# Hybrid attention layer: four of the output gate's eight row sums, and their weight loads, moved from z's second and fourth projection to its sixth and eighth

## The chip, the cores and the metric

The kernel runs on one core of one Trainium2 chip. The metric is the device time of one launch in microseconds (us), median of several runs. An execution taken by the hardware profiler gives the trace; its times count from the start of the span, which is the part of the launch that the trace covers. Engines are named as in the profile: PE (TensorE matmuls), PEld (its weight loads), DVE (VectorE), ACT (ScalarE), POOL (GpSimd), SP (SyncE, whose queue issues most DMAs). L764 is line 764 of the kernel before.

## The reference

One decoder layer on x of 512 tokens by 1024 features:

```
mod = silu(c) @ w_ada + b_ada ;  shift, scale, gate = split(mod, 3)
h = rms_norm(x, norm_gain) * (1 + scale) + shift
q_a,k_a,v_a,z_a, q_b,kc,vc,ks,vs,kw,vw, z_b,g_b = split(h @ w_in)
o_a = sliding-window attention (window 128, sinks) of group A, 8 heads
o_b = g0*compressed + g1*selected + g2*window-512 attention of group B, 8 heads
y = concat(o_a * silu(z_a), o_b * silu(z_b))
out = x + gate * (y @ w_out)
```

The change is about `gate`: 1024 numbers, each the dot product of silu(c) with one column of the last third of w_ada, plus its bias. They are needed only in the last line.

## The kernel before

Activations lie transposed, features on the 128 partitions, 512 tokens in a row. Every projection is made in split precision: a weight block is copied to a rounded high part `wh` (ACT, L192) and a low part `wl` (DVE, L193, weight minus `wh`), h likewise into `hh` and `hl`, and PE sums three products per block, `wh,hh`, `wl,hh` and `wh,hl` (L518 and L528). After a first stage that makes h and group A's q, k, v (to about 47 us), two things run beside each other and are interleaved on every engine:

- the **slots** of attention (`run`): 16 of group A, then 28 of group B (a slot is a pair of heads, a branch and a block of 128 queries). A slot is scores on PE (L1019 for A; L977 and L1004 for B, into PSUM tile `s`), bias and maximum on DVE (L1026; L979, L1006), exponential on ACT (L1010, L984), scaling (L1043, L1047 on DVE), transposes on PE (L1062, L1076, into `pt`), a copy on ACT (L1063, L1077), for group A a triangle mask on DVE (L1067, into `ptT`), and the product with the values on PE (L1095, into `po`), four slots at a time;
- the **stream** (`gen1`, then `gen2`): the other projections, in this order: kv_cmp, kv_sel, kv_win_g, q_b0, q_b1, then z in eight projections n = 0 to 7 (z_a0, z_a1, z_b0, z_b1, each in two halves of 128 columns). After q_b come norms and transposes for the queries of group B (`post_q`: L561 sums of squares, L114 to L121 an inverse root in small steps, L571 `qn`, L579 transposes on PE, L584 and L585 the halves `qs`).

Small pieces of work behind a projection (`posts`) are drawn one step at a time while the next projection is traced. One kind is `gate_slice(q)`: two DVE reductions (L764), each of a 128x1024 weight tile times the row `scrow` into one column of `gate`. Each starts at a raw weight tile and ends with `load_next()`.

Raw weights come through one pool `raw` of five buffers, in the fixed order `raw_order` (L160): a load for a tile goes to SP's queue and waits there until the tile five places before it has been used. What stands behind it in SP's queue waits too; among that are the bias rows of group B's heads (L966). The wh/wl pieces have four buffers each.

The order written in the code is not the final one: a scheduler places the instructions on each engine, and hoists what it thinks has time. `mark` keeps DVE instructions by name, and `in_order` ties later instructions behind one of them without a semaphore, that is, in the queue's order alone. The table `GATE` (L37) does this for the reductions n = 4 (behind `kn2`, the normalised window keys, L592) and n = 6 and 7 (behind `qn11`, the last L571).

The end (from about 256 us) is the output product, written out by hand in `TAIL`; the columns of `gate` are read there, first at 262 us.

Of the kernel before, what the change touches and what calls it, by code (L numbers as in the profile page):

```python
# [14 lines left out]
OP = mybir.AluOpType  # L15
# [18 lines left out]
NR = 4  # L34
LW = 4
PE_MODS = 2
GATE = {4: "kn2", 6: "qn11", 7: "qn11"}  # L37


TAIL = """  # L40
# [35 lines left out]
@contextmanager  # L76
def in_order(tc, after=(), only=None):

    traced = tc.nc.cur_bb.bb.instructions
    n = len(traced)  # L80
    last = dict(after)
    yield last
    info = mybir.DependencyInfo(mybir.DependencyClass.NoSync, mybir.DependencyReason.DATA)
    for i in tc.nc.cur_bb.bb.instructions[n:]:
        if only and i.engine not in only:
            continue
        if i.engine in last:
            tc.add_manual_dep(i, last[i.engine].name, info, reason="in_order")
        last[i.engine] = i
# [3 lines left out]
def hybrid_layer_kernel(ctx, tc, A, out):  # L93
    nc = tc.nc
    PE, DVE, ACT, POOL, SP = nc.tensor, nc.vector, nc.scalar, nc.gpsimd, nc.sync
# [14 lines left out]
    def rsqrt(v, n, name="n_y"):  # L110
# [15 lines left out]
    cT, prm, ident = first[:, 0:8], first[:, 8:40], first[:, 40:168]  # L126
# [30 lines left out]

    raw_order = [(g, h) for g in ("kv_cmp", "kv_sel", "kv_win_g") for h in range(2)]
    raw_order += [(f"cmp{kv}", q) for q in range(4) for kv in range(2)]
    raw_order += [(g, h) for g in ("q_b0", "gate0", "q_b1", "gate1", "z_a0", "gate2", "z_a1", "gate3", "z_b0", "z_b1",  # L160
                                   "o0", "o1", "o2", "o3") for h in range(2)]
    raws, pieces, pending = {}, {}, list(raw_order)

# [367 lines left out]
    chain, marks = {}, {}  # L531
# [227 lines left out]
    def gate_slice(q):  # L759

        for h in range(2):
            n, w = 2 * q + h, raws[f"gate{q}", h]
            with in_order(tc, {DVE.engine: marks[GATE[n]]} if n in GATE else {}, (DVE.engine,)):
                DVE.tensor_tensor_reduce(out=w, in0=w, in1=scrow, scale=0.5, scalar=prm[:, 16 + n:17 + n],  # L764
                                         op0=OP.mult, op1=OP.add, accum_out=gate[:, n:n + 1])
            load_next()
            yield 0.0

# [174 lines left out]
    def gen2():  # L943
        posts.append(cmp_attn())
        for n in range(8):
            b = PJ()
            yield from with_posts(unit_col(f"z_{'ab'[n // 4]}{n % 4 // 2}", n % 2, b))
            posts.insert(0, post_z(n, b))
            if n in (1, 3):
                posts.append(gate_slice(2 + n // 2))  # L950
        yield from flush_posts()


# [397 lines left out]
```

## Time and profile before

| what | value |
|---|---|
| time, 3 runs | median 299.51 us (299.44 to 300.15) |
| the profiled execution's own time | 299.99 us |
| its span in the trace | 297.7 us (2.29 us of the time lie around it) |
| PE busy | 290.1 us, 97% |
| PEld busy | 254.6 us, 86% |
| DVE busy | 261.0 us, 88% |
| ACT busy | 205.1 us, 69% |
| share of the chain that ended last | PE 70%, DVE 13%, DMA 10%, ACT 3% |
| the eight reductions L764 start at | 101.64, 103.76, 110.96, 114.10, 120.48, 132.56, 155.04, 169.97 us |

Granted clock of TensorE is full throughout. A PE matmul's busy time overlaps that of the next one, since they are pipelined; how far apart two matmuls start tells more than how long one is shown. Likewise a DVE instruction is shown some tens of ns longer than the step to the next start. In the timeline, a bracket behind a row gives the idle time before it and who ended it.

### The profile page before, as it was taken

To read this page: it belongs to the slowest core of one execution; us is meant where nothing else is said; L and a number is where in the kernel's file an instruction comes from. 1 tells how busy PE (TensorE), PEld (TensorE's weight loads), DVE (VectorE), ACT (ScalarE), POOL (GpSimd) and SP (SyncE) were. 2 spreads that over 40 slices of the span, in tenths; PEclk is the share of its full clock that TensorE was granted. 3 is DMA by queue.
4 is the path that set the end of the run, shared out by engine and by line. 5 is a ranking of instruction groups with operands and counts; after the bars stand their busy time and mean duration, and the time that the engine had idled before them with its cause. 6 is when DMAs were issued, how large, how long until landed. Compare 5 with 4: busy or idle time off the path is not lost.

```text
span 297.7 us, 6067 instructions
## 1 busy us (share of the span) xinstructions
PE 290.1 (97%) x2181; PEld 254.6 (86%) x2182; DVE 261.0 (88%) x730; ACT 205.1 (69%) x501; POOL 9.6 (3%) x28
## 2 busy tenths in 40 slices
PE   7999999999999999999999999999999999999995
PEld 3678888789989989989878988888888888889995
DVE  3689998999995998998999999999979779599992
ACT  5778657777848574967858567878877869567510
POOL 1000000000000100000000000000000000021210
PEclk9999999999999999999999999999999999999999
DMA  7999987842485884361402440223100120027272
GB/s 246 388 405 380 356 309 226 299 161 70 140 275 156 238 266 132 109 211 37 135 11 71 140 133 10 71 73 143 44 28 2 61 83 2 0 44 188 53 160 89
DMA packets 27417, 44.27 MB, mean 149 GB/s; under 512 B 1867, under 2 KB 18412, under 8 KB 27388
## 3 DMA queue, kind: packets, MB, share of 16 engines
q1 hardware_dynamic: 26380, 42.49, 42.2%
q0 software_dynamic: 864, 1.31, 3.0%
q8 instruction: 17, 0.28, 0.4%
q10 hardware_dynamic: 144, 0.09, 0.1%
q14 instruction: 12, 0.10, 0.1%
HBM read 41.74 MB, written 2.14 MB: 147 GB/s over the span
## 4 chain that ended last, share of the span: by engine, by line
PE 70%; DVE 13%; DMA 10%; ACT 3%; issue 2%; SPq 0%; DVEq 0%; ACTq 0%
PE pj L528 16%; PE pj L518 11%; PE po L1095 8%; PE pj L1205 6%; PE s L1004 5%; PE pt L1076 4%; DMA wst_ring<-in_w_qkv_a 4%; DMA ada_ring<-in_w_ada_rows 4%; PE s L1205 3%; PE pt L1062 3%; PE s L657 2%; DVE wl L193 2%; PE po L528 2%; DVE ada_ring L245 2%; PE s L1019 2%
## 5 line engine op out<-in xcount | busy, mean ns | idle before, releaser
L518 PE MATMUL pj<-wh,hh 128*128 128x256 f32 (+1 forms) x128 | 37.2, 291 | 0.0
L518 PE MATMUL pj<-wh,hl 128*128 128x256 f32 (+1 forms) x128 | 36.9, 288 | 0.0
L518 PE MATMUL pj<-wl,hh 128*128 128x256 f32 (+1 forms) x128 | 36.7, 287 | 0.0
L1010 ACT ACTIVATE pp<-pp,nm 128x256 f32<-128x256 f32 (+2 forms) x48 | 29.2, 610 | 6.3 <-DVE nm L1006 5.7
L528 PE MATMUL pj<-hh,wh 128*128 128x512 f32 x72 | 28.9, 402 | 0.0
L528 PE MATMUL pj<-hl,wh 128*128 128x512 f32 x72 | 28.8, 400 | 0.0
L528 PE MATMUL pj<-hh,wl 128*128 128x512 f32 x72 | 28.7, 399 | 0.0
L192 ACT ACTIVATE wh<-raw 128x512 fp32r<-128x512 f32 (+1 forms) x40 | 24.7, 635 | 5.3 <-PE pj L528 3.8
L193 DVE TENSOR_TENSOR wl<-raw,wh 128x512 fp32r<-128x512 f32 (+1 forms) x40 | 27.1, 692 | 1.4 <-ACT wh L192 1.1
L1006 DVE CUSTOM_DVE_ANT_0 pp<-s,bias 128x256 f32<-128x256 f32 (+2 forms) x48 | 25.5, 550 | 2.2 <-PE s L1004 2.0
L518 PEld LDWEIGHTS pj<-wh,hh 128*128 128x128 f32 x128 | 24.1, 189 | 0.4 <-issue 0.3
L518 PEld LDWEIGHTS pj<-wh,hl 128*128 128x128 f32 x128 | 24.2, 189 | 0.2 <-issue 0.2
L518 PEld LDWEIGHTS pj<-wl,hh 128*128 128x128 f32 x128 | 24.2, 189 | 0.1
L1004 PE MATMUL s<-kTb,qs 128*128 128x256 f32 (+2 forms) x96 | 23.6, 348 | 0.0
L1047 DVE TENSOR_SCALAR pp<-pp,rr,grev 128x256 f32<-128x256 f32 (+2 forms) x48 | 21.2, 474 | 0.3
L1004 PEld LDWEIGHTS s<-kTb,qs 128*128 128x128 f32 x96 | 16.9, 189 | 3.1 <-DVE nm L1006 0.3
L1010 ACT ACTIVATE pa<-pa,nm 128x129 f32<-128x129 f32 x32 | 12.7, 398 | 7.7 <-DVE nm L1026 6.0
L1077 ACT COPY ptT<-pt 128x384 f32<-128x384 f32 (+1 forms) x32 | 15.6, 526 | 1.1 <-PE pt L1076 1.0
L1063 ACT COPY ptT<-pt 128x256 f32<-128x256 f32 (+1 forms) x28 | 12.8, 457 | 4.1 <-PE pt L1062 3.7
L528 PEld LDWEIGHTS pj<-hh,wl 128*128 128x128 f32 x72 | 13.6, 188 | 2.4
L528 PEld LDWEIGHTS pj<-hl,wh 128*128 128x128 f32 x72 | 13.6, 189 | 2.3
L1076 PE MATMUL pt<-first,pp 128*128 128x128 f32 x112 | 15.5, 275 | 0.0
(320 smaller groups left out, 830.6 us busy)
## 6 DMA issues: line engine op xcount, KB each, us to landing
ada_ring<-in_w_ada_rows SPq DMA_DIRECT2D x12, 512.0 KB, 7.5
raw<-in_w_cmp SPq DMA_DIRECT2D x8, 512.0 KB, 6.6
raw<-in_w_gate SPq DMA_DIRECT2D x8, 512.0 KB, 4.5
raw<-in_w_o SPq DMA_DIRECT2D x8, 512.0 KB, 3.2
wst_ring<-in_w_qkv_a SPq DMA_DIRECT2D x8, 384.0 KB, 7.9
bias<-line_d SPq DMA_DIRECT2D x12, 256.0 KB, 4.0
xTp<-in_xT SPq DMA_DIRECT2D x8, 256.0 KB, 3.8
raw<-in_w_q_b SPq DMA_DIRECT2D x4, 512.0 KB, 4.8
```

Source lines behind the costliest of these rows:

```text
L192: ACT.activation(wh, src, AF.Copy)
L193: DVE.tensor_tensor(wl, src, wh.bitcast(F32), op=OP.subtract)
L518: PE.matmul(bank[:, t * n:(t + 1) * n], h[:, tb * 128:(tb + 1) * 128], w[:, k % 2, :], start=k == 0 and m == 0, stop=k == 7 and m == 2)
L528: PE.matmul(bank, w, h, start=k == 0 and m == 0, stop=k == 7 and m == 2)
L1004: PE.matmul(ps, qs[8 + 4 * g + r][:, 128 * i:128 * i + 128], kT[br, g][:, hl_, 0:w], start=hl_ == 0, stop=hl_ == 1)
L1006: DVE.tensor_tensor_reduce(out=P[:, g, 0:w], in0=ps, in1=bias["b", r, g][:, 512 - w:512], scale=1.0, scalar=3e38, op0=OP.add, op1=OP.min, ...
L1010: ACT.activation(P[:, g], P[:, g], AF.Exp, bias=nm[:, g:g + 1], scale=-1.0, accum_out=dn[:, g:g + 1])
L1047: DVE.tensor_scalar(v, v, rr[:, g:g + 1], gates[:, g, br:br + 1], op0=OP.mult, op1=OP.mult)
L1076: PE.transpose(pt[:, b * 128:(b + 1) * 128], P[:, g, b * 128:(b + 1) * 128], ident)
L1077: ACT.copy(T[:, 0:nb, :], rev(pt[:, 0:nb * 128].rearrange("p (b q) -> p b q", b=nb)))
L1095: PE.matmul(o[64 * g:64 * g + 64, 128 * i:128 * i + 128], vb[:, 64 * g:64 * g + 64], sl["T"][g][:, b, :], start=first_of and b == 0, stop= ...
L1205: PE.matmul(parts[g, p], a[:, r, :], b, start=new and r == 0 and m == 0, stop=r == 3 and m == 2, skip_group_check=True)
```

## The change

Three edits. In `raw_order` the tiles of gate2 and gate3 (four loads of 512 KB) move from between the z_a tiles to before and after z_b1. In `gen2` the two `gate_slice` calls that use them are put behind the projections n = 5 and n = 7 instead of n = 1 and n = 3. And the table GATE with its ties goes, so that all eight reductions stand where the scheduler puts them. No arithmetic changes, and the number of instructions of each kind stays the same.

```
-GATE = {4: "kn2", 6: "qn11", 7: "qn11"}
...
-    raw_order += [(g, h) for g in ("q_b0", "gate0", "q_b1", "gate1", "z_a0", "gate2", "z_a1", "gate3", "z_b0", "z_b1",
+    raw_order += [(g, h) for g in ("q_b0", "gate0", "q_b1", "gate1", "z_a0", "z_a1", "z_b0", "gate2", "z_b1", "gate3",
                                    "o0", "o1", "o2", "o3") for h in range(2)]
...
-            with in_order(tc, {DVE.engine: marks[GATE[n]]} if n in GATE else {}, (DVE.engine,)):
-                DVE.tensor_tensor_reduce(out=w, in0=w, in1=scrow, scale=0.5, scalar=prm[:, 16 + n:17 + n],
-                                         op0=OP.mult, op1=OP.add, accum_out=gate[:, n:n + 1])
+            DVE.tensor_tensor_reduce(out=w, in0=w, in1=scrow, scale=0.5, scalar=prm[:, 16 + n:17 + n],
+                                     op0=OP.mult, op1=OP.add, accum_out=gate[:, n:n + 1])
...
-            if n in (1, 3):
-                posts.append(gate_slice(2 + n // 2))
+            if n in (5, 7):
+                posts.append(gate_slice(n // 2))
```

In the changed kernel the lines stand one to two lower: the reduction is L762 there, L1067 is L1065, L518 is L517, L1004 is L1002. Up to DVE's `kn2` all engines' orders are the same as before. Behind it they part; from the instructions on that before came at about 237 us of the trace they are the same again, up to numbers of buffers.

First place: DVE behind `kn2` (`kn` in the first row), and the PE instruction that waits there. `ss_q` are sums of squares for group B's queries, `s` and `pa` belong to group A's slots. Before:

```order
L592 TENSOR_TENSOR kn<-kr,n_y 128x512
L1051 TENSOR_SCALAR pa<-pa,rr 128x128
L764 ISA raw,gate<-raw,scrow,first 128x1024
L764 ISA gate 128x1
L1043 RECIPROCAL rr<-dn 128x2
L561 TENSOR_REDUCE ss_q<-sq 128x8
L1051 TENSOR_SCALAR pa<-pa,rr 128x128
```

and now:

```order
L591 TENSOR_TENSOR kn<-kr,n_y 128x512
L1049 TENSOR_SCALAR pa<-pa,rr 128x128
L1041 RECIPROCAL rr<-dn 128x2
L1049 TENSOR_SCALAR pa<-pa,rr 128x128
L560 TENSOR_REDUCE ss_q<-sq 128x8
L1021 COPY_PREDICATED s<-rest,s 128x2x128
```

The fifth reduction is gone from here, and likewise the sixth from the small steps of q_b0's inverse root, in front of L115. The last mask product L1067 of these slots stood nine instructions behind the one before it (a masked copy L1023, four low parts, two maxima L1026 and two pieces of the window keys, L606); now one low part and one maximum lie between. On PE the last product with `va_step`, which reads its `ptT`, stood before behind eleven matmuls of q_b1's projection:

```order
L518 MATMUL pj<-wh,hh_83 128x256
L518 MATMUL pj<-wl,hh_83 128x256
L518 MATMUL pj<-wh,hl_91 128x256
L518 MATMUL pj<-wh,hh_84 128x256
L518 MATMUL pj<-wl,hh_84 128x256
L518 MATMUL pj<-wh,hl_92 128x256
L518 MATMUL pj<-wh,hh_85 128x256
L518 MATMUL pj<-wl,hh_85 128x256
L518 MATMUL pj<-wh,hl_93 128x256
L518 MATMUL pj<-wh,hh_86 128x256
L518 MATMUL pj<-wl,hh_86 128x256
L1095 MATMUL po<-ptT,va_step 64x128 x2
```

Now it is ahead of them:

```order
L1093 MATMUL po<-ptT,va_step 64x128 x2
L1093 MATMUL po<-ptT,va 64x128 x2
L1093 MATMUL po<-ptT,va_step 64x128 x2
L517 MATMUL pj<-wh,hh_83 128x256
L517 MATMUL pj<-wl,hh_83 128x256
```

Second place: DVE at q_b1's inverse root (`n_t`, `n_y`), between two low parts (`wl`) of z_a1. Before:

```order
L117 SCALAR_TENSOR_TENSOR n_y<-n_t,n_y 128x16
L118 TENSOR_TENSOR n_t<-n_y 128x16
L119 SCALAR_TENSOR_TENSOR n_t<-n_t,ss_q 128x16
L193 TENSOR_TENSOR wl<-raw,wh 128x512
L120 SCALAR_TENSOR_TENSOR n_t<-n_t 128x16
L121 SCALAR_TENSOR_TENSOR n_y<-n_t,n_y 128x16
L571 TENSOR_TENSOR qn<-pp,n_y 128x512 x2
```

Now the fifth reduction stands among them:

```order
L116 SCALAR_TENSOR_TENSOR n_y<-n_t,n_y 128x16
L117 TENSOR_TENSOR n_t<-n_y 128x16
L118 SCALAR_TENSOR_TENSOR n_t<-n_t,ss_q 128x16
L762 ISA raw,gate<-raw,scrow,first 128x1024
L762 ISA gate 128x1
L192 TENSOR_TENSOR wl<-raw,wh 128x512
L119 SCALAR_TENSOR_TENSOR n_t<-n_t 128x16
L120 SCALAR_TENSOR_TENSOR n_y<-n_t,n_y 128x16
L570 TENSOR_TENSOR qn<-pp,n_y 128x512 x2
```

The sixth stands where the eighth stood before (169.97 us of the trace). The seventh and the eighth stand behind two reciprocals L1043 of group B's second pair of heads, which before came at 189.45 and 195.71 us. So the scheduler has hoisted all four to places well ahead of the projection behind which the code puts them.

Third place: PE at the scores of group B's first 256-wide slot (two pairs, one for each key group, into the two buffers of `s`). Before, the second pair came behind the end of q_b1's projection (L518) and nine matmuls of z's first (L528), the last seven of them these:

```order
L1004 MATMUL s<-kTb_657,qs_1812 128x256 x2
L528 MATMUL pj<-hh_82,wl 128x512
L528 MATMUL pj<-hh_83,wh 128x512
L528 MATMUL pj<-hl_91,wh 128x512
L528 MATMUL pj<-hh_83,wl 128x512
L528 MATMUL pj<-hh_84,wh 128x512
L528 MATMUL pj<-hl_92,wh 128x512
L528 MATMUL pj<-hh_84,wl 128x512
L1004 MATMUL s<-kTb_659,qs_1815 128x256 x2
```

Now thirteen matmuls of q_b1 are still to come when it stands:

```order
L1002 MATMUL s<-kTb_657,qs_1812 128x256 x2
L517 MATMUL pj<-wh,hh_85 128x256
L517 MATMUL pj<-wl,hh_85 128x256
L1002 MATMUL s<-kTb_659,qs_1815 128x256 x2
L517 MATMUL pj<-wh,hl_93 128x256
```

The two pairs, and ahead of them the transposes L579 (by twelve matmuls of q_b1's projection) and the scores L977 (by nine), have moved forward in PE's queue. On DVE the four maxima L979 in front of the first 256-wide slot stood before with four low parts `wl` between or ahead of them; now these low parts come behind. In the second pair of heads (about 187 to 210 us) it is the other way round: there PE has up to thirteen more of z's matmuls ahead of the same transposes L1076 than before.

On SP's queue the loads of gate2 and gate3 now stand among those of z_b. The bias rows of the third pair of heads (L966) stood before behind the first load of w_o; now they stand behind the third of these four loads, and the fourth behind them.

## The prediction

> **What bounds the kernel now.** I read the page's busy times and its chain first, then the busy times of the stretch in which the change acts, then the timeline of PE there, and last the lists of who waited for whom.
>
> ```profile
> PE 290.1 (97%) x2181; PEld 254.6 (86%) x2182; DVE 261.0 (88%) x730; ACT 205.1 (69%) x501; POOL 9.6 (3%) x28
> PE 70%; DVE 13%; DMA 10%; ACT 3%; issue 2%; SPq 0%; DVEq 0%; ACTq 0%
> ```
>
> The busy times from 120 us (the fifth reduction) to 231 us (PE, PEld, DVE, ACT, POOL, then clock and DMA):
>
> ```profile
> 120.00:231.00 111.00, 110.36 (x851) 96.41 (x850) 105.64 (x323) 83.99 (x219) 0.60 (x3) 1.00 0.25 81
> ```
>
> PE is busy for 110.36 of 111 us, DVE for 105.64, so neither number alone settles which one sets the pace: matmuls overlap in this view. What settles it is how far apart they start. Three stretches of PE's timeline, at 129, at 151 and in the tail, where the chain holds nothing but PE:
>
> ```profile
> 129.47 0.28 PE L518 MATMUL pj<-wh,hh 128*128 128x256 f32 x1
> 129.59 0.28 PE L518 MATMUL pj<-wl,hh 128*128 128x256 f32 x1
> 130.17 0.44 PE L1095 MATMUL po<-ptT,va_step 128*64 128x128 f32 x4 [0.30 <-DVE ptT L1067]
> ...
> 151.50 0.39 PE L528 MATMUL pj<-hh,wl 128*128 128x512 f32 x1
> 151.73 0.40 PE L528 MATMUL pj<-hh,wh 128*128 128x512 f32 x1
> 152.20 0.33 PE L579 MATMUL pt<-first,qn 128*128 128x128 f32 x1
> ...
> 264.57 0.28 PE L1205 MATMUL pj<-yh,woh 128*128 128x256 f32 x1
> 264.69 0.28 PE L1205 MATMUL pj<-yl,woh 128*128 128x256 f32 x1
> ```
>
> A 256-column matmul takes 0.12 us from start to start (129.47 to 129.59), and the same in the tail (264.57 to 264.69). A 512-column one takes 0.23 (151.50 to 151.73). So between its waits PE runs at the pace that it has where nothing holds it, and only a PE wait that goes can shorten the program. Two stand after 120 us and behind the fifth reduction: 129.59 to 130.17 is 0.58 in place of 0.12, 0.46 lost; 151.73 to 152.20 is 0.47 in place of 0.23, 0.24 lost. The waits name who was late:
>
> ```profile
> PE po L1095 <- DVE ptT L1067: 0.3, 1, 0.3
> PE pt L600 <- DVE kn L592: 0.3, 1, 0.3
> ```
>
> ```profile
> PEld pt L579 <- DVE qn L571: 0.5, 1, 0.5
> ```
>
> The wait for `kn` lies ahead of the change. In sum 0.46 + 0.24 = 0.70 us can be had behind it.
>
> **The change part by part.** The arithmetic is the same, so it is a matter of places only.
>
> *Two reductions leave the stretch from 120 to 134 us.* DVE there:
>
> ```profile
> 120.48 1.28 DVE L764 CUSTOM_DVE_ANT_0 raw<-raw,scrow,first 128x1024 f32<-128x1024 f32 x1
> 121.69 0.16 DVE L1043 RECIPROCAL rr<-dn 128x2 f32<-128x2 f32 x1
> ...
> 129.69 0.42 DVE L1067 TENSOR_TENSOR ptT<-ptT,rest 128x256 f32<-128x256 f32 x1
> ...
> 132.56 1.28 DVE L764 CUSTOM_DVE_ANT_0 raw<-raw,scrow,first 128x1024 f32<-128x1024 f32 x1
> ...
> 135.66 1.29 DVE L571 TENSOR_TENSOR qn<-pp,n_y 128x512 f32<-128x512 f32 x2
> ```
>
> A reduction holds DVE from 120.48 to 121.69, 1.21 us. Without the fifth, the mask product at 129.69 comes 1.21 us earlier and, since more work moves behind it, earlier still: at 128.48 at the latest. PE now asks for it eleven matmuls sooner, 130.17 less the 0.46 wait less 11 x 0.12 = 128.39. It needs to be done 0.34 us after its start, so the fifth's absence alone would not do. The new order does: of the nine instructions ahead of it, three low parts among them now come behind, and a low part alone is 0.6 us (below, 143.48 to 144.69 for two). Three are 1.8 us, so it starts by 126.7 and is done at 127.0, 1.4 us ahead. This wait goes: **-0.46**.
>
> *The sixth goes from the front of `qn`.* With both reductions out, `qn` comes at most 2 x 1.21 = 2.42 us earlier, and 1.21 if DVE then waits for the data of PE that now comes no earlier. Its reader, the transposes L579, has moved twelve matmuls up, 12 x 0.12 = 1.42, and by the 0.46 saved: 1.88. Before, the first half of `qn` was done at 136.27 and the reader came at 136.44, a slack of 0.17 by these rows:
>
> ```profile
> 136.27 0.68 DVE L571 TENSOR_TENSOR qn<-pp,n_y 128x512 f32<-128x512 f32 x1
> 136.44 0.62 PE L579 MATMUL pt<-first,qn 128*128 128x128 f32 x4
> ```
>
> So the new slack is 0.17 + 2.42 - 1.88 = +0.71, or 0.17 + 1.21 - 1.88 = -0.50. A wait of 0 to 0.50 us; I take **+0.2**, nearer to none, since DVE's list of waits from 120 to 136 us holds a single one, of 0.2 us:
>
> ```profile
> DVE s L1023 <- PE s L1019: 0.2, 1, 0.2
> ```
>
> *The scores of group B move up on PE.* The four maxima that free `s` for the second pair of L1004, and the rows that they stand among:
>
> ```profile
> 140.78 0.69 DVE L193 TENSOR_TENSOR wl<-raw,wh 128x512 fp32r<-128x512 f32 x1
> ...
> 142.56 0.69 DVE L193 TENSOR_TENSOR wl<-raw,wh 128x512 fp32r<-128x512 f32 x1
> ...
> 143.48 1.29 DVE L193 TENSOR_TENSOR wl<-raw,wh 128x512 fp32r<-128x512 f32 x2
> 144.69 0.28 DVE L979 CUSTOM_DVE_ANT_0 pp<-s,bias 128x128 f32<-128x128 f32 x1
> 144.89 0.28 DVE L979 CUSTOM_DVE_ANT_0 pp<-s,bias 128x128 f32<-128x128 f32 x1
> ```
>
> ```profile
> 145.00 0.28 PE L1004 MATMUL s<-kTb,qs 128*128 128x256 f32 x1
> ```
>
> That pair moves up by thirteen L518 and nine L528, 13 x 0.12 + 9 x 0.23 = 3.6 us. The last of the four starts at 144.89 and ends at 145.1, so it too was just in time. It gains 1.21 to 2.42 from the reductions and 4 x 0.60 = 2.4 from the low parts that now stand behind it, 3.6 to 4.8 in all. That covers 3.6. I take 0; the rival below has the case where it doesn't. The low parts themselves are wanted by z's first projection, which comes behind the thirteen L518, in its old place.
>
> *The fifth comes back ahead of q_b1's `qn`,* now reading a tile that SP may only fetch when z_a0's fourth low part has freed a buffer. Fetches of such tiles, in the middle and at their shortest and longest:
>
> ```profile
> raw<-in_w_gate SPq DMA_DIRECT2D x8, 512.0 KB, 4.5
> ```
>
> ```profile
> raw<-in_w_gate SPq DMA_DIRECT2D x1, 512.0 KB, 3.3
> ```
>
> ```profile
> raw<-in_w_gate SPq DMA_DIRECT2D x1, 512.0 KB, 5.5
> ```
>
> Between that low part and the reduction DVE has almost the same instructions as it had between these rows:
>
> ```profile
> 146.22 0.65 DVE L561 TENSOR_REDUCE ss_q<-sq 128x8 f32<-128x512 f32 x1
> 146.79 1.11 DVE L1040 TENSOR_SCALAR pp<-pp,rr,grev 128x128 f32<-128x128 f32 x4
> ...
> 150.43 0.69 DVE L193 TENSOR_TENSOR wl<-raw,wh 128x512 fp32r<-128x512 f32 x1
> ```
>
> It is one L1040 less (1.11 / 4 = 0.28), so 4.21 - 0.28 = 3.93 us. DVE waits 0 (3.3) to 1.57 us (5.5), 0.57 at the middle value; queued behind it are a low part and `qn`, for which PE waited 0.24 before. `qn` has a lead of 2.42 - 1.21 = 1.21 left, PE comes 0.26 earlier by the terms above, and has two L528 more in front, 0.47. Its lateness is 0.24 - 1.21 + 0.26 - 0.47 = -1.18: on time by 1.18 with no wait on DVE, and by 0.61 with 0.57. That old wait goes: **-0.24**; a slowest load gives back 1.57 - 1.18 = 0.39. The Trainium skill, in "DMA: Bandwidth & Descriptors", section Anatomy of one DMA — SWDGE (gpsimd) path, fits 2.0 us plus bytes over 436 GB/s, which as an estimate is 3.2 us for 512 KB: the fifth would not wait; it is fitted for another issuing path, and the median here is 4.5.
>
> *The seventh and eighth* go from 155.04 and from 169.97 (now the sixth's place) to the reciprocals that came at 189.45 and 195.71, 2.42 us of DVE work in a stretch where DVE is nearly full:
>
> ```profile
> 180.00:200.00 20.00, 20.00 (x138) 16.69 (x137) 19.53 (x64) 15.89 (x43) 0.00 (x0) 1.00 0.15 53
> ```
>
> ```profile
> 189.45 0.16 DVE L1043 RECIPROCAL rr<-dn 128x2 f32<-128x2 f32 x1
> ...
> 195.71 0.16 DVE L1043 RECIPROCAL rr<-dn 128x2 f32<-128x2 f32 x1
> ```
>
> Up to there DVE has done two reductions fewer than before, and behind 197 us as many. PE has up to thirteen more z matmuls in front of the transposes there, 13 x 0.23 = 3.0 us. They hide the two; without them the cost would be what DVE lags, up to 1.2. I take 0.
>
> *SP's queue.* z_b's loads are released earlier, gate2's and gate3's later. The bias rows of the third pair of heads go behind the third gate load; when they were issued before, how long such a load takes, and who reads them:
>
> ```profile
> 175.34 1.52 SPq L966 DMA_DIRECT2D bias<-line_d  x2
> ```
>
> ```profile
> bias<-line_d SPq DMA_DIRECT2D x12, 256.0 KB, 4.0
> ```
>
> ```profile
> 206.35 0.29 DVE L979 CUSTOM_DVE_ANT_0 pp<-s,bias 128x128 f32<-128x128 f32 x1 [0.23 <-PE s L977]
> ```
>
> They may come 206.35 - 175.34 - 4.0 = 27 us later before anyone waits. Nothing.
>
> The sum: -0.46 + 0.20 - 0.24 = -0.50. The profiled execution took 299.99 us, 297.7 in the span and 2.29 around it; it becomes 299.49. It lies 0.48 above the median of the runs, 299.51, so the forecast is 299.51 - 0.50 = **299.0**. A measurement of this kernel can tell about 0.3%, 0.9 us, from no change: "same" is 298.6 to 300.4.
>
> **The rivals.**
>
> *It moves nothing that counts* (299.5). The sixth reduction ends up where the eighth stood and the fifth only 28 us later, so the change does but half of what its code says, and the two PE waits may be replaced by equal ones: the new wait at L579 at its 0.50 and 0.2 for the slow load. For it: each wait that goes lets PE run up to the next late operand. Against: three of the margins above are over 0.6 us.
>
> *Scores too early* (slower). PE, an engine in strict order, asks for the second pair of L1004 3.6 us sooner. If the low parts behind the maxima don't help, because it is the chain from `qn` over transposes, ACT's and DVE's halves `qs` and back that sets the maxima, the maxima come only 1.21 to 2.42 sooner, and PE stands for 3.6 - 2.42 = 1.2 to 2.4 us; the -0.70 + 0.20 remain: 299.0 + 1.2 to 2.4 = 300.2 to 301.4, in the middle 300.8. For it: in the trace the last maximum ends just when PE comes, and the four `qs` are made in turn on two engines. Against: the 2.4 us of low parts between the maxima, which the rows above show back to back with them. It decides from the point where the fourth maximum ends later than 145.1 - 3.6 - 0.26 = 141.2 us.
>
> *DVE is the real bound* (faster). If PE's 99% is only overlap and DVE at 105.64 of 111 us sets the pace up to the slots' end, two reductions out of the stretch ahead of group B's start let everything behind run 2.42 us sooner, and the DVE idle time that is left later takes them in: 299.5 - 2.42 = 297.1. Against it stand the matmul starts, 0.12 and 0.23 apart as in the tail. The Trainium skill, in "Perfetto Trace Analysis", section Identifying the Most-Contended Engine, says that matmul busy time is a poor measure and that weight-load busy time should be used with the use of peak flops; by it PE is at 96.41 of 111, 87%, DVE at 95%, and the most contended engine would be DVE. The trace does not bear it out as far as start distances go.
>
> **How the numbers follow.** The forecast, waits gone and small ones left, has 0.57; nothing that counts 0.10; scores too early 0.20; DVE the bound 0.13. Forecast and first rival lie within 0.3%, but for 0.02 of the forecast, where no new wait comes at L579 and other small ones fall too. Of the slow rival nearly all lies above 300.4. So faster 0.15, same 0.65, slower 0.20. The forecast's own range is 298.8 (no new wait) to 299.4 (0.50 at L579 and a little at the slow load). The range reaches up into the slow rival, to 301.0, which leaves 0.05 above, and down to 298.4, some of the way to 297.1, which leaves 0.11 below.
>
> **What would show it.** Right: L1095 without a wait for L1067 near 128 us, L579 near 151 us without one for `qn`, at most 0.5 us at the first L579, and starts 0.12 and 0.23 apart everywhere else. The slow rival: over 1 us of PE at L1004 for `nm` of L979 near 141 us. The fast one: starts closer than 0.12 and 0.23, or the tail's first matmul over 2 us earlier. Wrong on the load: DVE stands over 1.2 us in front of the fifth reduction, and PE behind it at L579.

## The result and the profile after

The changed kernel takes 301.39 us (median of 6, 300.72 to 301.74), the kernel before 299.55 in its six runs: ratio 1.0058, 95% interval 1.0048 to 1.0069. It is slower by 1.7 us where the forecast was 0.5 us faster. Its profiled execution took 301.39 us as well, 299.1 of it in the span.

The page's busy times and the chain that ended last, after:

```profile
PE 290.3 (97%) x2182; PEld 254.6 (85%) x2182; DVE 262.0 (88%) x730; ACT 205.3 (69%) x501; POOL 9.6 (3%) x28
PE 61%; DVE 18%; DMA 8%; ACT 7%; issue 3%; SPq 0%; ACTq 0%; DVEq 0%
```

The work is the same, but the chain runs over PE for 61% of the span in place of 70%, and over DVE and ACT for 25% in place of 16%. The same stretch as in the prediction, after:

```profile
120.00:231.00 111.00, 109.04 (x827) 95.22 (x829) 103.90 (x312) 83.13 (x213) 0.57 (x3) 1.00 0.25 80
```

Every engine is idle for a little longer. PE's waits behind 118 us, after:

```profile
PE pt L578 <- DVE qn L570: 1.2, 2, 0.8
PE pt L599 <- DVE kn L591: 0.3, 1, 0.3
PE s L1002 <- ACT pp L846: 0.3, 1, 0.3
PE pj L527 <- ACT ptT L1061: 0.2, 1, 0.2
PE s L1002 <- DVE nm L1004: 0.2, 1, 0.2
```

The wait for the mask product is gone, as forecast. In its place PE waits for `qn` at both transposes (L579 before, L578 now). The starts around the three largest stalls, after:

```profile
133.64 0.28 PE L517 MATMUL pj<-wh,hh 128*128 128x256 f32 x1
133.76 0.28 PE L517 MATMUL pj<-wl,hh 128*128 128x256 f32 x1
134.81 0.33 PE L578 MATMUL pt<-first,qn 128*128 128x128 f32 x1 [0.77 <-DVE qn L570]
...
145.34 0.51 PE L1002 MATMUL s<-kTb,qs 128*128 128x384 f32 x2
146.11 0.44 PE L1002 MATMUL s<-kTb,qs 128*128 128x384 f32 x1 [0.26 <-ACT pp L846]
...
152.62 0.40 PE L527 MATMUL pj<-hh,wl 128*128 128x512 f32 x1
153.44 0.33 PE L578 MATMUL pt<-first,qn 128*128 128x128 f32 x1 [0.43 <-DVE qn L570]
```

From start to start, less the pace of the matmul in front, PE loses 1.05 - 0.12 = 0.93 us at q_b0's transposes, 0.42 at the scores of 384 columns (the pair's second matmul starts at 145.51), and 0.82 - 0.23 = 0.59 at q_b1's transposes. Three smaller stalls follow, 0.21 at 160.8, 0.36 at 162.1 and 0.35 at 199.1. Elsewhere the starts are 0.12 and 0.23 apart, as before.

Where DVE was when. The last window keys `kn` are the last instruction of DVE whose place did not change; before and after:

```profile
119.68 0.69 DVE L592 TENSOR_TENSOR kn<-kr,n_y 128x512 f32<-128x512 f32 x1
```

```profile
119.24 0.69 DVE L591 TENSOR_TENSOR kn<-kr,n_y 128x512 f32<-128x512 f32 x1
...
134.07 1.29 DVE L570 TENSOR_TENSOR qn<-pp,n_y 128x512 f32<-128x512 f32 x2
...
150.47 1.28 DVE L762 CUSTOM_DVE_ANT_0 raw<-raw,scrow,first 128x1024 f32<-128x1024 f32 x1 [0.57 <-DMA raw<-in_w_gate]
...
152.69 1.29 DVE L570 TENSOR_TENSOR qn<-pp,n_y 128x512 f32<-128x512 f32 x2
```

The traces differ by 0.44 us ahead of any change, so times are counted from `kn` below. From `kn` to q_b0's `qn` it was 15.98 us (135.66 - 119.68) and is 14.83: two sums of 1.21 us went out and 1.15 us were won. From there to q_b1's `qn` it was 15.79 (151.45 - 135.66) and is 18.62: one sum came in and 2.83 were lost. The tail's first matmul, row 264.57 of the prediction, is now this one:

```profile
265.99 0.28 PE L1203 MATMUL pj<-yh,woh 128*128 128x256 f32 x1
```

From `kn` that is 144.89 before and 146.75 after, 1.86 us: the whole slowdown, and 1.68 of it stands already at q_b1's `qn` (31.77 before, 33.45 after).

The first part's missing 1.27 us lie where the fifth sum was. DVE's key parts `kTb` and the later of q_b0's two `ss_q`, before:

```profile
122.68 1.50 DVE L606 SCALAR_TENSOR_TENSOR kTb<-pt,kgain,kTb 64x512 fp32r<-64x512 f32 x2
...
130.44 0.67 DVE L561 TENSOR_REDUCE ss_q<-sq 128x8 f32<-128x512 f32 x1
```

and after, with the wait that DVE has in front of the key parts:

```profile
120.45 0.17 DVE L1041 RECIPROCAL rr<-dn 128x2 f32<-128x2 f32 x1 [0.33 <-ACT pa L1008]
...
122.41 1.50 DVE L605 SCALAR_TENSOR_TENSOR kTb<-pt,kgain,kTb 64x512 fp32r<-64x512 f32 x2
...
130.43 0.68 DVE L560 TENSOR_REDUCE ss_q<-sq 128x8 f32<-128x512 f32 x1
```

The key parts come 3.00 us behind `kn` before and 3.17 after: with 1.21 us less in front of them they are not earlier at all. ACT, which makes its share of them first, starts 1.60 behind `kn` in both (121.28 and 120.84). In the sum's place stand the wait of 0.33 for ACT's exponential, and a masked copy and a maximum that came behind the key parts before (121.57 and 122.14 us). The busy times of the two stretches (third pair of figures: DVE), before and after:

```profile
119.68:122.68 3.00, 2.72 (x24) 2.55 (x23) 2.95 (x9) 2.96 (x10) 0.23 (x1) 1.00 0.81 238
```

```profile
119.24:122.41 3.17, 2.90 (x25) 2.72 (x25) 2.63 (x9) 3.13 (x10) 0.19 (x1) 1.00 0.28 84
```

DVE is idle for 0.05 us of the first and 0.54 of the second. At the later `ss_q` it is 11.19 us behind `kn` in place of 10.76, still no earlier; all of the gain comes between there and `qn`, 3.64 us in place of 5.22, where the sixth sum was. Between the two `qn` DVE's waits, after:

```profile
DVE qs L584 <- ACT qs L583: 0.8, 1, 0.8
DVE raw L762 <- DMA raw<-in_w_gate: 0.6, 1, 0.6
DVE ss_q L560 <- ACT sq L556: 0.5, 1, 0.5
```

Before there was only the first of these, of 0.7 us. The second is the fifth sum's tile, from its issue to its landing in the chain of waits, after:

```profile
145.30 5.14 DMA raw<-in_w_gate
```

### The profile page after: what moved, and what is told of

It is laid out like the page before. It is cut to its first block, busy times and chain, and to the rows that moved or that the text cites. A ratio compares the mean times of both kernels' runs of the same rounds, so it can differ in the third digit from the quotient of the medians.

```text
span 299.1 us, 6082 instructions
## 1 busy us (share of the span) xinstructions
PE 290.3 (97%) x2182; PEld 254.6 (85%) x2182; DVE 262.0 (88%) x730; ACT 205.3 (69%) x501; POOL 9.6 (3%) x28
## 4 chain that ended last, share of the span: by engine, by line
PE 61%; DVE 18%; DMA 8%; ACT 7%; issue 3%; SPq 0%; ACTq 0%; DVEq 0%
PE pj L527 15%; PE po L1093 7%; PE pj L517 7%; PE pj L1203 6%; PE s L1002 5%; PE pt L1074 4%; DVE ada_ring L244 4%; PE s L1203 3%; DMA raw<-in_w_gate 3%; DMA ada_ring<-in_w_ada_rows 3%; PE s L656 2%; DVE wl L192 2%; PE pt L1060 2%; DMA ada_ring<-in_w_ada_cols 2%; PE po L527 2%
## 5 line engine op out<-in xcount | busy, mean ns | idle before, releaser
L517 PE MATMUL pj<-wh,hh 128*128 128x256 f32 (+1 forms) x128 | 37.2, 291 | 0.0
L517 PE MATMUL pj<-wl,hh 128*128 128x256 f32 (+1 forms) x128 | 36.8, 287 | 0.0
L517 PE MATMUL pj<-wh,hl 128*128 128x256 f32 (+1 forms) x128 | 36.7, 286 | 0.0
L1004 DVE CUSTOM_DVE_ANT_0 pp<-s,bias 128x256 f32<-128x256 f32 (+2 forms) x48 | 25.5, 548 | 2.2 <-PE s L1002 2.0
L517 PEld LDWEIGHTS pj<-wh,hh 128*128 128x128 f32 x128 | 24.1, 188 | 0.4 <-issue 0.3
L1002 PE MATMUL s<-kTb,qs 128*128 128x256 f32 (+2 forms) x96 | 23.9, 349 | 0.5 <-ACT pp L846 0.3
L517 PEld LDWEIGHTS pj<-wl,hh 128*128 128x128 f32 x128 | 24.2, 189 | 0.1
L517 PEld LDWEIGHTS pj<-wh,hl 128*128 128x128 f32 x128 | 24.1, 189 | 0.0
L1002 PEld LDWEIGHTS s<-kTb,qs 128*128 128x128 f32 x96 | 16.6, 188 | 3.6 <-ACT pp L846 0.6
L527 PEld LDWEIGHTS pj<-hh,wh 128*128 128x128 f32 x72 | 13.5, 188 | 3.0 <-ACT ptT L1061 0.6
```

What stands on the lines that cost most here:

```text
L517: PE.matmul(bank[:, t * n:(t + 1) * n], h[:, tb * 128:(tb + 1) * 128], w[:, k % 2, :], start=k == 0 and m == 0, stop=k == 7 and m == 2)
L527: PE.matmul(bank, w, h, start=k == 0 and m == 0, stop=k == 7 and m == 2)
L1002: PE.matmul(ps, qs[8 + 4 * g + r][:, 128 * i:128 * i + 128], kT[br, g][:, hl_, 0:w], start=hl_ == 0, stop=hl_ == 1)
L1004: DVE.tensor_tensor_reduce(out=P[:, g, 0:w], in0=ps, in1=bias["b", r, g][:, 512 - w:512], scale=1.0, scalar=3e38, op0=OP.add, op1=OP.min, ...
```

## The experiments

Three theories were on record. **1:** PE's new order asks for the chain of group B sooner than DVE can deliver, and this costs by itself. **2:** the fifth sum's late tile, and its place in front of q_b1's `qn`, cost. **3:** the seventh and eighth cost where they now stand. Several kernels hold an engine's instructions in a given order, by ties without semaphores written behind the program (`hold`, shown once below); the list of places is left out of the diffs. The columns of the table: median, ratio to the kernel before on the same chip with its interval; then from the profiled execution, counted from `kn`, the start of q_b0's `qn`, of q_b1's `qn`, and of the tail. In the profiled executions of e1, e2, e10 and e11 the granted clock fell for a while (last section), which can make the tail of these four, and both `qn` of e2, later as well.

| kernel | median us | ratio (95%) | q_b0 | q_b1 | tail |
|---|---|---|---|---|---|
| before | 299.55 | 1 | 15.98 | 31.77 | 144.89 |
| after | 301.39 | 1.0058 (1.0048 to 1.0069) | 14.83 | 33.45 | 146.75 |
| e4 gate3 only | 299.41 | 0.9987 (0.9979 to 0.9996) | 15.97 | 31.76 | 144.96 |
| e8 no ties | 299.99 | 1.0027 (1.0013 to 1.0041) | 15.97 | 33.68 | 145.52 |
| e6 two sums out, PE of before | 299.01 | 0.9984 (0.9976 to 0.9993) | 14.51 | 31.39 | 144.59 |
| e7 two sums out | 300.13 | 1.0020 (1.0011 to 1.0029) | 14.82 | 30.97 | 145.57 |
| e3 late sums tied | 301.09 | 1.0050 (1.0037 to 1.0062) | 14.84 | 31.13 | 146.28 |
| e9 six buffers | 300.52 | 1.0033 (1.0021 to 1.0046) | 14.83 | 32.79 | 146.20 |
| e13 transposes later | 301.43 | 1.0059 (1.0043 to 1.0075) | 14.84 | 33.25 | 146.72 |
| e14 both | 301.01 | 1.0044 (1.0031 to 1.0058) | 14.84 | 32.82 | 146.39 |
| e2 before, PE of after | 302.43 | 1.0098 (1.0081 to 1.0114) | 17.46 | 33.61 | 147.86 |
| e1 after, PE of before | 304.43 | 1.0163 (1.0144 to 1.0181) | 14.52 | 33.67 | 150.80 |
| e5 tied, PE of before | 301.78 | 1.0081 (1.0069 to 1.0093) | 14.52 | 31.54 | 147.40 |
| e12 all sums late | 301.89 | 1.0080 (1.0068 to 1.0092) | 14.52 | 31.54 | 147.91 |
| e10 first part PE of before | 306.77 | 1.0236 (1.0222 to 1.0251) | 15.08 | 37.36 | 152.06 |
| e11 the same, six buffers | 305.94 | 1.0216 (1.0203 to 1.0229) | 15.06 | 36.66 | 151.62 |
| e15 two DVE moves | 299.48 | 0.9994 (0.9983 to 1.0004) | 15.98 | 31.27 | 145.06 |

### Which part of the change

**e4, only the last pair moved.** Against before:

```
-GATE = {4: "kn2", 6: "qn11", 7: "qn11"}
+GATE = {4: "kn2"}
...
-    raw_order += [(g, h) for g in ("q_b0", "gate0", "q_b1", "gate1", "z_a0", "gate2", "z_a1", "gate3", "z_b0", "z_b1",
+    raw_order += [(g, h) for g in ("q_b0", "gate0", "q_b1", "gate1", "z_a0", "gate2", "z_a1", "z_b0", "z_b1", "gate3",
...
-            if n in (1, 3):
-                posts.append(gate_slice(2 + n // 2))
+            if n in (1, 7):
+                posts.append(gate_slice({1: 2, 7: 3}[n]))
```

> The kernel before with only the last pair of loads and sums moved behind z's eighth projection (no ties for these two); the fifth and sixth stay at their old places, and PE's order up to the first scores of group B is that of before. Theory 1 and theory 2: nothing is lost, 299.2 to 299.8. Theory 3: the seventh and eighth cost what they lag, 300.0 to 300.8.

299.41 us, ratio 0.9987: nothing lost. Theory 3 falls for the last pair by itself, though not at the changed kernel's places: the seventh and eighth start 55.4 and 71.8 us behind `kn` here, 74.4 and 80.6 there. The gain of a tenth of a per cent is at the edge of what can be told, and from `kn` to the tail nothing was won (144.96 beside 144.89). It is the only version here that does the whole computation and has its interval below 1.

**e8, only the ties off.** Against before:

```
-GATE = {4: "kn2", 6: "qn11", 7: "qn11"}
+GATE = {}
```

> The kernel before with its three ties taken off and nothing else: loads and the places of the sums in the code are those of before. All orders but SP's are those of the changed kernel with tied sums. Theory 1: the ties alone hold PE's order, so without them it is 300.9 to 301.4, as long as with the moved loads. Theory 2 (the load that comes late): 299.3 to 299.8, since no load is moved.

The expectation rested on a wrong reading of the order: without ties the fifth and sixth sum and the first transposes keep their places, and it is the seventh and eighth that move forward, to 18.8 and 31.0 us behind `kn`. So the run says nothing on theory 1. It shows another thing: with two sums more in front of q_b1's `qn`, one of them among its small steps and its tile long there, `qn` comes at 33.68 in place of 31.77, as late as in the changed kernel, and yet only 0.5 us are lost. PE doesn't wait at q_b1's transposes here; it waits for maxima (`nm`), 0.3 us at 146 and 0.2 at 161. So what a late `qn` costs depends on where PE's readers stand.

**e7 and e6, the fifth and sixth sum left out** (two columns of the gate are set to zero, their tiles still loaded), once with the scheduler free, once with PE held in the order of before. Against before:

```
+    POOL.memset(gate[:, 4:6], 0.0)
...
+            if n not in (4, 5):
```

and, to hold an order, this function (`order` is the list of places; e6, e1, e2, e5 and e12 have its loop written out, for PE alone):

```
+def hold(tc, engine, order):
+    n, words = order
...
+            if last is not None:
+                tc.add_manual_dep(traced[k], last.name, info, reason="in_order")
+            last = traced[k]
```

> The kernel before without the fifth and sixth sum (left out, as in the run beside this one), everything placed anew by the scheduler, which puts PE's instructions up to the first scores of group B in the order of the changed kernel. Theory 1: although DVE has 2.4 us less to do, PE loses the 0.93 and 0.42 us of the changed kernel, 300.3 to 301.2, slower than before. Theory 2 alone (the late load and the place of the fifth sum): 299.0 or less.

> The kernel before without the fifth and sixth sum (two of the eight are left out and their columns set to zero; their tiles are still loaded), PE's instructions held in the order of the kernel before. Forecast's bound: PE sets the pace, two sums less on DVE are worth the two PE waits at most, 298.8 to 299.4. Rival, DVE sets the pace: 2.4 us less, 297.1 to 297.6.

With 2.4 us less to do on DVE e7 is slower than before by 0.6 us, a little less than theory 1 had it, and e6 faster by 0.5. The two differ in what the hold of PE's order brings with it and in nothing else. PE's waits in e7 behind 118 us:

```profile
PE pt L580 <- DVE qn L572: 0.8, 1, 0.8
PE s L1006 <- ACT pp L850: 0.3, 1, 0.3
PE pt L601 <- DVE kn L593: 0.3, 1, 0.3
```

and in e6:

```profile
PE pt L616 <- DVE kn L608: 0.3, 1, 0.3
PE pt L595 <- DVE qn L587: 0.2, 1, 0.2
```

e7 has the changed kernel's first two stalls (0.92 and 0.44 from start to start) without any late sum or late tile. So these two stalls need no late sum; they come with the new order, and between e6 and e7 that order costs 1.1 us. It is not shown that PE's part of it alone does: with PE held the scheduler places DVE's instructions otherwise too. e6 also measures what two sums on DVE are worth where PE keeps its order: 0.5 us of 2.4 (0.2 to 0.7 by the interval). That this gives the forecast's 299.0 is chance, since the forecast was for a kernel that still makes the sums. The rival with DVE as the only bound (297.1) falls.

### The late tile

**e3, the late sums tied behind the last `qn`.** Against after:

```
+            with in_order(tc, {DVE.engine: marks["qn11"]} if n > 3 else {}, (DVE.engine,)):
```

> The changed kernel, with its four late reductions tied behind the last qn, so that none stands in front of q_b1's qn. Up to the first scores of group B PE's order is that of the changed kernel; behind them q_b1's transposes stand eight matmuls further up. Theory 2: the 0.6 us lost at q_b1's transposes goes, 300.8 or less. Theory 1: the 0.93 and 0.42 us stay, and the transposes, asked for sooner, still wait: 300.9 to 301.6.

301.09, in theory 1's range, though not with the wait that theory 1 still had at q_b1's transposes: `qn` comes at 31.13, sooner than before, and the 0.59 us there are gone, as theory 2 had it. But of 1.86 us from `kn` to the tail 1.39 remain: 0.93 and 0.41 at the old two places, and 0.32 and 0.20 us at 160.7 and 196.7, in front of which the sums now stand.

**e9, six raw buffers**, all orders held as in the changed kernel. Against after (and `hold` for PE, DVE and ACT):

```
-    rawp = ctx.enter_context(tc.tile_pool(name="rawp", bufs=5))
+    rawp = ctx.enter_context(tc.tile_pool(name="rawp", bufs=6))
```

> The changed kernel with PE's, DVE's and ACT's instructions held in its own order, and six raw buffers in place of five, so that every fetch is released one tile earlier. Theory 2 (the fifth sum's tile, fetched late, holds q_b1's qn): DVE's 0.57 us in front of the fifth sum goes, and with it most of PE's 0.59 at q_b1's transposes, while the 0.93 and 0.42 ahead stay: 300.7 to 301.0. Theory 1 alone (PE's order moved ahead of DVE's chain): the late tile is hidden anyway, 301.2 to 301.6.

300.52, a little below theory 2's range: the ratio goes from 1.0058 to 1.0033, and from `kn` to the tail it is 0.55 us less. The late tile is a cause, shown. PE's waits in it: q_b1's transposes are gone from the list, the others stand.

```profile
PE pt L630 <- DVE qn L622: 0.9, 1, 0.9
PE pt L651 <- DVE kn L643: 0.3, 1, 0.3
PE s L1054 <- ACT pp L898: 0.3, 1, 0.3
PE pj L579 <- ACT ptT L1113: 0.2, 1, 0.2
PE s L1054 <- DVE nm L1056: 0.2, 1, 0.2
```

### Is it PE's order alone?

**e2, the kernel before with PE held as in the changed kernel.** Against before: `hold` for PE.

> The kernel before, loads, ties and places of the gate sums untouched, with PE's instructions held in the order that they have in the changed kernel. Theory 1: PE asks for qn about 2 us earlier than before while DVE has both reductions in front of it, so it stands about 2 us there and the time is 301.3 to 302. Theories 2 and 3: the loads and the late reductions are those of before, so nothing is lost, 299.3 to 299.8.

302.43, a little over theory 1's range (three of its five executions lie between 301.94 and 302.43), with the loss at another reader than expected: PE now asks for the last mask product eleven matmuls sooner, and DVE still has both sums.

```profile
129.52 0.44 PE L1110 MATMUL po<-ptT,va_step 128*64 128x128 f32 x4 [1.79 <-DVE ptT L1082]
```

**e1, the changed kernel with PE held as before**, and **e5**, the same with the sums tied as in e3. Against after (and e3): `hold` for PE.

> The changed kernel, with PE's instructions held in the order that they have in the kernel before; DVE, ACT and SP are placed anew, the four late reductions stay late. Theory 1 (PE's order: the scheduler moves the reads of group B's first chain up by 1.4 to 3.6 us, and DVE's chain gains only about 1.2): the wait at the first transposes L579 (0.93 us lost in the changed kernel) and at the scores L1004 near 145 us (0.42) go, so 301.4 - 1.35 = 300.0 or less, down to 299.2 if the old wait for the mask product goes too. Theory 2 (the fifth reduction's late load and its place among the small steps of q_b1's inverse root): little changes, 300.8 to 301.5, and PE still loses about 0.6 us at q_b1's transposes. Theory 3 (the seventh and eighth reduction in the full stretch behind 180 us): 301 or more, with the loss behind 160 us.

> The changed kernel with its late sums tied behind the last qn (as in the run before) and PE's instructions held in the order of the kernel before. Theory 1 (PE's order moved ahead of DVE's chain) and theory 2 (the fifth sum, fetched late, in front of q_b1's qn) have both lost their cause here, so the 0.46 and 0.23 us that the forecast counted on are to be had: 298.9 to 299.4. Theory 3 (the late sums in the full stretch behind 155 us): 300 or more, with PE waits behind 155 us.

Both were expected near 299 to 300 by theory 1, and came out at 304.43 and 301.78. The first transposes no longer wait in either. But the scheduler places the late sums anew against the held order, in e1 the fifth ahead of all small steps of q_b1's root, and PE stands at q_b1's transposes:

```profile
154.06 0.66 PE L593 MATMUL pt<-first,qn 128*128 128x128 f32 x4 [2.45 <-DVE qn L585]
```

In e5 a late sum (at 154.1 us) stands ahead of maxima that PE needs at 160 us, and PE loses 1.04 us there and 0.56 at 210. So the order of before does not bring back the time of before as long as DVE has the two sums behind 134 us. Theory 1 is not the whole cause.

**e10 and e11, only the first part of PE's order as before** (to the scores of 384 columns), DVE and ACT held as in the changed kernel, with five and six buffers.

> The changed kernel with DVE's and ACT's instructions held in its own order; PE's are held in the order of the kernel before from the last mask product's reader up to the first scores of 384 columns (near 146 us) and from there in the changed kernel's. Theory 1 as a sum of waits: the 0.93 and 0.42 us go, 300.0 or less. Theory of two limits side by side (PE's order asks too early, and the fetch of the fifth sum's tile sets when q_b1's qn can come, whatever PE does): the two first waits go, the one at q_b1's transposes grows from 0.6 to about 1.5 to 2 us, and the time stays at 300.8 to 301.8.

> Both of the two runs beside this one: PE's first part in the order of the kernel before, and six raw buffers; DVE and ACT held in the changed kernel's order. Two limits side by side: with both gone the waits at the first transposes, at the scores and most of that at q_b1's transposes go, and more is won than by the two apart: 299.6 to 300.4. What is left over 299.5 is the place of the sums behind 150 us (theory 3).

306.77 and 305.94, far outside. PE's waits in e10:

```profile
PE pt L631 <- DVE qn L623: 3.6, 1, 3.6
PE pj L580 <- DVE wl L245: 1.1, 1, 1.1
```

The changed kernel's DVE makes the four low parts behind the maxima; PE's old order wants the first low part between the two pairs of scores that these maxima read. Each engine's order fits only the other's, so these two runs don't price theory 1.

**e13 and e14, the first transposes eight matmuls later** on PE, all else held as in the changed kernel, with five and six buffers. The diff against after is `hold` with nine entries of PE's list behind eight others.

> The changed kernel, PE, DVE and ACT held in its own order, but with q_b0's two groups of transposes (where PE lost 0.93 us) eight projection matmuls later, 8 x 0.12 = 0.94 us, so that PE does these in place of waiting. If the waits add up: 301.4 - 0.93 = 300.5. If the chain of qn, qs, maxima, low parts, fetch and q_b1's qn sets the time behind it: PE comes 0.93 us sooner to the next readers and stands there, 301.2 to 301.6, with more than the 0.6 us of the changed kernel at q_b1's transposes.

> The same with six raw buffers, so that the fifth sum's tile comes in time (that alone gave 300.52). If the waits add up: 300.5 - 0.93 = 299.6. If the chain over qs and the maxima holds PE even without the late tile: 300.3 to 300.6, with the wait at the scores (0.42) or at q_b1's transposes grown.

301.43 and 301.01. In e13 the stall of 0.93 us is gone, and this is what the list of PE's waits has in its place:

```profile
PE pt L630 <- DVE qn L622: 0.8, 1, 0.8
PE s L1027 <- DVE qs L636: 0.6, 1, 0.6
PE pt L651 <- DVE kn L643: 0.3, 1, 0.3
```

PE does the eight matmuls, comes to the transposes at the same moment (15.60 us behind `kn`, 15.57 in the changed kernel), and then has none left to put under the scores of group B (0.73 lost) and under q_b1's transposes (0.94). The waits don't add up: the time that PE doesn't lose at one reader it loses at the next. That is the chain's account, as expected. In e14 the waits moved in the same way (0.6 us at the scores, 0.3 at q_b1's transposes), but its time is above the 300.3 to 300.6 expected; it lies 0.2 us behind e9 from `kn` to the tail, and the intervals of the two ratios overlap.

### Two more

**e12, all four sums behind z's last projection**, tied behind group B's third pair's first maxima, PE held as before. Against after:

```
-    raw_order += [(g, h) for g in ("q_b0", "gate0", "q_b1", "gate1", "z_a0", "z_a1", "z_b0", "gate2", "z_b1", "gate3",
+    raw_order += [(g, h) for g in ("q_b0", "gate0", "q_b1", "gate1", "z_a0", "z_a1", "z_b0", "z_b1", "gate2", "gate3",
...
+            with in_order(tc, {DVE.engine: marks["both2"]} if n > 3 else {}, (DVE.engine,)):
...
-            if n in (5, 7):
-                posts.append(gate_slice(n // 2))
+            if n == 7:
+                posts.extend((gate_slice(2), gate_slice(3)))
...
+        mark(f"both{r}")
```

> The changed kernel with all four late sums (and their loads) moved once more, behind z's last projection, and tied behind the first maxima of the third pair of heads (near 206 us in the trace of before), where DVE has idle time again; PE's instructions held in the order of the kernel before. If the sums cost by falling into DVE's full stretch from 140 to 200 us, none does here, and the forecast's gain is to be had: 298.7 to 299.2, like the run with two sums left out (299.0). If moving them late costs in itself (w_o's loads come later): 299.8 or more.

301.89. Up to q_b1's `qn` it is as good as before (31.54), and the 3.0 us from `kn` to the tail are lost later; the longest wait, 1.0 us, ends at 245.96 us:

```profile
PE pt L1091 <- DVE pp L1062: 1.0, 1, 1.0
```

DVE's idle time behind 206 us is no free room either; whether w_o's later loads or the sums themselves push that piece was not told apart.

**e15, e4 with two DVE instructions exchanged with neighbours**: the last mask product ahead of a key part and a maximum, and a low part from in front of q_b1's first half of `qn` to behind it. The diff against e4 is `hold` for PE, DVE and ACT, with these two entries moved in DVE's list.

> The kernel with only the last pair of sums moved (299.41 beside 299.78 for the kernel before), all orders held, and two DVE instructions exchanged with their neighbours: the last mask product one place ahead of the key part and the maximum in front of it, and one low part from in front of q_b1's first qn half to behind it. If PE sets the pace but for its two waits (0.46 and 0.21): 299.4 - 0.6 = 298.8. If other work is late at once behind them: 299.2 to 299.5.

299.48 beside 299.69 for before, no difference that can be told, and none to e4 from `kn` to the tail (145.06 and 144.96). The two waits of 0.46 and 0.21 us are gone; the list of waits has the reason:

```profile
PE pt L652 <- DVE kn L644: 0.3, 1, 0.3
PE pt L631 <- DVE qn L623: 0.2, 1, 0.2
```

PE came 0.46 sooner to q_b0's transposes and lost 0.34 there from start to start, then 0.20 and 0.19 near 157 us. So the forecast's two waits are worth nothing by themselves here.

## Why the prediction was wrong

**The wait for the mask product, -0.46:** it went, as worked out. **What it is worth** was the first error, in the part on the bounds: "only a PE wait that goes can shorten the program" is true, but I took it the other way round too, each wait for its size. e15 took away both waits and won nothing; e13 took away 0.93 us and won nothing.

**The first transposes, +0.2 (0 to 0.50):** the step that failed. It measured 0.93. I gave `qn` up to 2.42 us and leaned to that end because DVE's list of waits held one entry. That list can't tell what DVE would wait for without the sums: with the fifth gone DVE's key parts came 3.17 us behind `kn` in place of 3.00, behind a wait for ACT and two instructions pulled ahead, and the fifth's 1.21 us brought nothing to `qn`. `qn` gained 1.15, just under my lower end of 1.21; PE's place moved by 136.44 - 120.52 = 15.92 against (133.76 + 0.12) - 120.08 = 13.80, 2.12 us in place of 1.88; and the slack was 0.17 - 0.13, since PE starts 0.13 behind the end of a `qn` half (134.07 + 0.61 to 134.81). 0.04 + 1.15 - 2.12 = -0.93.

**The scores of group B, 0:** the second pair of 256 columns had no wait over 0.1 us, so the cover of 3.6 to 4.8 was there: the third maximum ended at 140.07, 20.83 us behind `kn` in place of 25.21, 4.38 sooner. The fourth, by which I meant to judge the rival, doesn't free that pair: PE started it at 141.22 and the fourth maximum only came at 141.33. The slot behind it lost 0.42, for ACT's copy L846 of q_b1's projection; I had not looked at that engine's order.

**The fifth sum, -0.24:** DVE's wait was 0.57 us, the forecast's middle value to the digit, but by luck: the tile took 5.14 us and not 4.5, and DVE was ready for it 5.2 us behind the low part that ended at 144.68, not 3.93. (The estimate of 3.2 us by the Trainium skill's fit in "DMA: Bandwidth & Descriptors", section Anatomy of one DMA — SWDGE (gpsimd) path, which is fitted for another issuing path, is not what this queue gave.) What failed is "`qn` has a lead of 2.42 - 1.21 = 1.21 left": the lead had gone at the first transposes, whose halves `qs` DVE and ACT make in turn, and `qn` came 1.68 late. PE was short by 0.59, not ahead by 0.61. e9 prices the late tile at 0.55 us from `kn` to the tail, 0.75 us by the ratios.

**The seventh and eighth, 0, and SP's queue, 0:** e4 bears out the first for places somewhat earlier; behind the seventh PE loses 0.35 us at 199.1 in the changed kernel, and no run prices that alone. No row after shows a wait for a bias.

**The rivals.** "It moves nothing that counts" missed the time, but its reason, that a wait that goes lets PE run up to the next late operand, is what e13 and e15 show. "Scores too early" had the sign and the time (300.2 to 301.4, 300.8) and the reason, PE's order ahead of DVE's, but not the place: PE waited twice for `qn`, not over 1 us for the maxima. "DVE is the real bound" was too much: e6 shows 0.5 us of 2.4. What I lacked was a rival in which a sum that is taken out brings nothing where it stood.

**An account, and what stays open.** From `kn` to the tail three kernels divide the 1.86 us: 0.68 are there with two sums left out and the scheduler free (e7, 145.57), 0.63 more with all four late sums where the changed kernel has them and their tiles in time (e9, 146.20), and 0.55 more with the late tile (after, 146.75). By the ratios to before it is 0.20, 0.13 and 0.25%. Only the last step differs in one thing; the middle one also moves the seventh and eighth sum and the loads. So a third of the loss or a little more is the late tile, shown, and another third comes with the new order even where DVE has less to do; which engine's part of that order costs is not shown. How much of the first two stalls would remain if PE's order were mended and the tile came in time is open: each attempt to hold one engine's order against another's (e1, e5, e10, e11) broke the schedule elsewhere.

## What to carry to other kernels

Work in an engine's queue may be filling time in which that engine would wait: before you count its removal as a gain, follow the next instruction's input back to the engine that makes it, since the list of waits can't show a wait that is filled. Where two engines are both nearly full (here 99 and 95% of the stretch), a stall removed on one can come back at its next reader of the other, as in e13 and e15; count the length of the chain between two fixed points, and not the sum of its stalls. A scheduler that is given freedom moves more than the step that was freed, so compare all engines' orders, and price the places where a reader moved further than what it reads.

## What the runs showed of the hardware

After a wait of about 2 us on PE the clock that it is granted can fall to half for a while. Windows of e2's profiled execution around its stall (127.46 to 129.52 from start to start) and behind it; of the last three figures the first is the granted clock:

```profile
130.00:132.00 2.00, 2.00 (x11) 2.00 (x12) 2.00 (x8) 1.77 (x6) 0.00 (x0) 0.56 1.08 371
132.00:134.00 2.00, 2.00 (x13) 2.00 (x13) 0.63 (x4) 0.41 (x1) 0.00 (x0) 0.59 0.25 100
134.00:136.00 2.00, 2.00 (x19) 2.00 (x18) 1.65 (x11) 0.53 (x3) 0.00 (x0) 1.00 0.00 0
```

From 130.2 to 133.6 us the 256-column matmuls of e2 start 0.21 apart in place of 0.12, about 1.5 us more lost than the stall itself. The profiled executions of e1, e10 and e11, with waits of 2.45, 3.6 and 2.8 us, have it too, at 0.50 in their slowest 2 us. Stalls of 1.41 us (e10 at 144 us) and less, all of the changed kernel's among them, left the clock at 1.00. It does not come in every execution: of five each, two of e2 (303.15 and 303.27 us) and two of e1 (305.50 and 305.81) have a mean granted clock of 0.994, the other three 1.000 (301.94 to 302.43 and 303.96 to 304.43); all nine of e10 and e11 have 0.994 or less. So the medians of e1 and e2 hold none of it, and of the distance of e10 and e11 from what was expected it is a part, about 1.5 us for a stretch like e2's. What decides between the executions of one kernel is not shown. The Trainium skill, in "TensorE: Matmul & The Clock Gate", section Part 1: The HAM clock gate (the "warmup" mystery), has the half rate set in after an idle window of about 3.4 us; here a wait of 1.79 us by the profile was enough in the profiled execution of e2, and the slow stretch lasted about 3.4 us.
